# Weight low parts on GpSimd in two halves, softplus high parts on ScalarE, and a rotary table applied earlier, in a two-block transformer kernel

## The chip, the cores and the metric

The kernel runs on 1 core of one Trainium2 chip. The metric is the device time of the whole program in microseconds. Before the change three runs gave 2197.65, 2197.91 and 2201.13 us, a median of 2197.91 us.

## What is computed

Two transformer blocks run one after the other on 512 tokens of width 1024, in float32. Cut to what matters here:

```python
# first block
h = x + 0.5 * swiglu(rms_norm(x))                       # 1024 -> 2816 -> 1024
u = rms_norm(h) @ w_in                                  # q_lat, kv_lat, k_rope, qd, kd, vd
q = (rms_norm(q_lat) @ w_q_up)                          # 8 heads of 64 plain + 32 rotary columns
q_nope = rms_norm(q[..., :64]) ; q_rot = apply_rope(rms_norm(q[..., 64:]), cos, sin)
o_mla = softmax(q @ k.T * scale) @ v                    # first mixer, 8 heads, beside 4 heads of
h = h + concat(o_mla, o_diff) @ w_out                   # difference attention
h = h + 0.5 * swiglu(rms_norm(h)); h = h + gate * rms_norm(p @ w_ple_proj)
# second block, 16 meta tokens ahead of the 512
z = qa @ ka.T * scale                                   # stick breaking, 8 heads
log_keep = where(strict, log_sigmoid(-z), 0)            # = -softplus(z) below the diagonal
a = exp(log_sigmoid(z) + (reverse_cumsum(log_keep) - log_keep)) @ va
# beside it top-k sparse attention, then a mixture of 32 experts, top 2
```

## The kernel before, in words

**Two parts for each factor.** A float32 product is made on TensorE as three products of rounded parts: high by high, high by low and low by high (`mm3`, lines 393 to 397). Each operand is split into a high part, which is the value rounded to the matmul's type, and a low part, which is the value less the high part. For weights this is `wload` (lines 371 to 380): SyncE starts the transfer of a 128 by 1024 block, ScalarE writes the high part (line 376) and GpSimd and VectorE by turns subtract it (line 379). Three raw blocks and three split blocks are held at a time, and `stream` (line 997) loads one weight block ahead of its use. For activations it is `split` (lines 382 to 391).

**Stages.** First feed-forward (to about 385 us of the span), first mixer (to about 720), second feed-forward (to about 1065), a gated projection (to about 1155), second mixer (to about 1600), output projection, and the experts (from about 1670). In a mixer two programs are woven by `merge` (line 1025): the attention, and a stream of projections of 24 products each. A planner then orders the instructions of each engine by program order and by its own estimates of cost and readiness, and puts in the semaphores. Each engine works through its own queue in that order.

**First mixer.** `t_mla` (line 689) projects one pair of heads, gets four tiles `y` from PSUM on VectorE (line 614) and hands three of them to `row_rstd` (line 469), where ScalarE squares them, TensorE sums the squares and VectorE refines the inverse root. Later `mla_n` (line 835) normalises: `kn` (line 840), and for each of the two heads `mqn` (line 848), then the product of its 64 rotary rows with the table `rtab` (line 849), then the split into high part (ScalarE) and low part (GpSimd). The scores follow in `mla_s` (line 856).

**Second mixer.** `sb_a` (line 1359) takes the scores of one head in three groups, two of 512 columns and one of 256. ScalarE copies them (line 1369) and makes Abs, Exp and Ln (lines 1372 to 1374), VectorE adds the positive part (line 1375), GpSimd masks the diagonal blocks (lines 1349 and 1351), VectorE writes the high part (line 1383), GpSimd the low part (line 1384). `sb_b` (line 1390) sums both parts on TensorE (line 1401) and adds the copied scores on VectorE (line 1403). Between these, VectorE runs the top-k of the sparse attention, 64 rounds of a maximum and a replacement (lines 1326 and 1327), woven in by `rank`.

Of the kernel before, what the change touches and what calls it, by code (L numbers as in the profile page):

```python
# [8 lines left out]
F32 = mybir.dt.float32  # L9
F32R = mybir.dt.float32r  # L10
I32 = mybir.dt.int32
AF = mybir.ActivationFunctionType
OP = mybir.AluOpType
# [223 lines left out]
class Prog:  # L237
# [133 lines left out]
    def wload(self, ap, n=1024):  # L371
        nc = self.nc
        raw = self.raw()
        nc.sync.dma_start(raw, ap)
        hl = self.ws.tile([P, 2, 1024], F32R, name="whl", tag="ws")
        nc.scalar.activation(hl[:, 0, :n], raw[:, :n], AF.Copy)  # L376
        e = nc.vector if self.lo_i % 2 else nc.gpsimd
        self.lo_i += 1
        e.tensor_sub(hl[:, 1, :n], raw[:, :n], hl[:, 0, :n].bitcast(F32))  # L379
        return hl  # L380

    def split(self, hl, src, scale=None, rows=slice(0, P), cols=slice(None), lo=None):
# [168 lines left out]
    def block1(self):  # L551
        nc, I = self.nc, self.I
# [17 lines left out]
        rtab = self.U("rtab")  # L570
# [27 lines left out]
        def proj(w, evac=None, src=None, kc=KC, o=0):  # L598
            ps = self.G()
            for k in range(kc):  # L600
                c = slice(o + k * P, o + k * P + P)
                x = (xs if src is None else src)[k]
                self.mm3(ps, w[:, 0, c], w[:, 1, c], x[:, 0, :], x[:, 1, :], k == 0, k == kc - 1)
                if k % 2:
                    yield 1.3
            if evac is None and "rb" not in L_:
                L_["first"] = ps
                return
            evacuate(ps, L_["rb"] if evac is None else evac)
# [6 lines left out]
        def mark(key, lag=0.0):  # L616
            done[key] = self.clock + lag

        def stats(key, items):
            L_[key] = self.row_rstd(items)  # L620
            mark(key, LAG)
# [67 lines left out]
        def t_mla(w, p):  # L689
            if p % 2 == 0:  # L690
                L_["wq"] = w
            ql = [L_["ql", 0], L_["ql", 1]]
            ys = []
            for e in range(2):
                yield from proj(L_["wq"], L_["rbq"], ql, 2, ((2 * p + e) % 4) * 256)
                ys.append(L_["y"])
            for o in (0, 512):
                yield from proj(L_["wkv"], L_["rbkv"], [L_["kvl"]], 1, o + p * P)
                ys.append(L_["y"])
            yield 1.3  # L700
            vd["m", p] = self.U("vm")
            self.transposes(vd["m", p], ys[3])
            Y_["m", p] = ys
            stats(("m", p), [(ys[0], 1), (ys[1], 2), (ys[2], 0)])
            yield 2.0

        def t_wkv(w, _):
# [30 lines left out]
        def need(key):  # L738
            while key not in done or self.clock < done[key]:
                yield None  # L740
# [94 lines left out]
        def mla_n(p):  # L835
            yield from need(("m", p))
            ys, r = Y_.pop(("m", p)), L_["m", p]
            es = [self.pairs(r, 6, o) for o in (4, 0, 2)]
            kn = self.U("kn")
            nc.vector.scalar_tensor_tensor(kn, ys[2], self.g1[:, GMKN : GMKN + 1], self.bc2(es[0]), op0=OP.mult, op1=OP.mult)  # L840
            yield 0.4
            q_["m", p], k_["m", p] = [], []
            for e in range(2):
                rn, rr = slice(64 * e, 64 * e + 64), slice(64 * (1 - e), 64 * (1 - e) + 64)
                k = L_["kt"][e][p % 2]
                self.split(k, kn[rn], rows=rn, lo=nc.gpsimd)
                t = self.U("mqn")
                nc.vector.scalar_tensor_tensor(t, ys[e], gs[:, e : e + 1], self.bc2(es[1 + e]), op0=OP.mult, op1=OP.mult)
                nc.vector.tensor_tensor(t[rr], t[rr], rtab[rr], op=OP.mult)
                q = self.HL("mq")  # L850
                self.split(q, t, lo=nc.gpsimd)
                q_["m", p].append(q)
                k_["m", p].append(k)
                yield 0.4
# [48 lines left out]
        for k in range(2):  # L903
            raw = self.U("praw")
            nc.scalar.dma_start(raw, I["pT"][k])
            hl = self.HL("pT")
# [9 lines left out]
        for h in range(4):  # L916
            for s, f in enumerate((t_q, t_k, t_v)):
                T_["qkv"[s] + str(h)] = [(wA[3 * h + s], lambda w, f=f, h=h: f(w, h))]
            T_[f"m{h}"] = [(I["w_qup"][h // 2] if h % 2 == 0 else None, lambda w, h=h: t_mla(w, h))]
            T_[f"wo{h}"] = [(I["w_out"][h, m4], lambda w, h=h, m4=m4: t_wo(w, h, m4)) for m4 in range(2)]  # L920
# [158 lines left out]
    def mixer2(self):  # L1079
        nc, I = self.nc, self.I  # L1080
# [17 lines left out]
        def need(key):  # L1098
            while key not in done or self.clock < done[key]:
                yield None  # L1100
# [245 lines left out]
        def dmask(t, g):  # L1346
            if g == (1, 3):
                t3 = t.rearrange("p (b c) -> p b c", b=4)[:, 0:4:3, :]
                nc.gpsimd.tensor_tensor(t3, t3, mask.unsqueeze(1).to_broadcast([P, 2, P]), op=OP.mult)
            else:  # L1350
                nc.gpsimd.tensor_tensor(t[:, :P], t[:, :P], mask, op=OP.mult)

        def zmm(z, p, e, j):
            qa, kp = qa_[p], kp_[p]
            r = slice(64 * e, 64 * e + 64)
            kc = slice(j * P, j * P + P)
            self.mm3(z, kp[r, 0, kc], kp[r, 1, kc], qa[r, 0, j * P :], qa[r, 1, j * P :], True, True)

        def sb_a(h):

            p, e = h // 2, h % 2
            yield from need(("ka", p))
            for g in GR:
                w = W[g]
                z = self.PS()
                for j in g:
                    zmm(z[:, OFF[j] : OFF[j] + T - j * P], p, e, j)
                zc = self.U("zc")[:, :w]
                nc.scalar.copy(zc, z[:, :w])
                zz[h, g] = zc  # L1370
                t = self.U("sp")[:, :w]
                nc.scalar.activation(t, z[:, :w], AF.Abs)
                nc.scalar.activation(t, t, AF.Exp, scale=-1.0)
                nc.scalar.activation(t, t, AF.Ln, bias=self.ones)
                nc.vector.scalar_tensor_tensor(t, z[:, :w], 0.0, t, op0=OP.max, op1=OP.add)
                dmask(t, g)
                if w == 512:
                    s = self.HL("spl")
                    hi, lo = s[:, 0, :], s[:, 1, :]
                else:  # L1380
                    s = self.U("splz", 512, F32R)
                    hi, lo = s[:, :256], s[:, 256:]
                nc.vector.tensor_copy(hi, t)
                nc.gpsimd.tensor_sub(lo, t, hi.bitcast(F32))
                for j in g:
                    c = slice(OFF[j], OFF[j] + T - j * P)
                    spl[h, j] = (hi[:, c], lo[:, c])
                yield w * 0.00128
# [167 lines left out]
        def attention():  # L1556
            yield from idx()
            self.tc.keep_in_program_order(nc.scalar.preload_act_table_set("natural_log_exp_and_others"))
            yield from sb_a(0)
            for h in range(8):  # L1560
                p, e = h // 2, h % 2
                g = [sb_a(h + 1)] if h < 7 else []
                g.append(sb_b(h))
                if e == 0 and p:
                    g += [sb_sum(p - 1), sb_o(p - 1)]
                for d in self.zip_(*g):
                    yield d
                    rank(1)
                rank(3)
                if h == 7:  # L1570
                    yield from sb_meta()
            yield from self.zip_(sb_sum(3), sb_o(3))
            yield from sb_meta2()
            rank(80)
            yield from ds_s(0)
            for p in range(4):
                g = [ds_o(p)]
                if p < 3:
                    g.insert(0, ds_s(p + 1))
                if p == 0:  # L1580
                    g.append(sb_out())
                yield from self.zip_(*g)
            self.dump("yb", [t[:, 0, :].bitcast(F32) for t in yb])
# [561 lines left out]
```

## Time and profile before

| | |
|---|---|
| median of three runs | 2197.91 us |
| the profiled execution | 2201.16 us |
| its span, first to last instruction | 2199.3 us |
| mean granted TensorE clock | 0.980 |
| busy: TensorE, VectorE, ScalarE, GpSimd | 2115.3, 1012.4, 707.7, 517.4 us |

Busy time is an average over stages with different limits, so a stage has to be read from its own windows. A busy time includes the time in which an instruction has started and cannot go on. Idle time is put down to the event that came last before it ended. The clock column of a window gives the granted TensorE clock as a share of full speed.

### The profile page before, as it was taken

What the parts mean: (1) busy time and instruction counts of PE and PEld (TensorE: products, weight loads), DVE (VectorE), ACT (ScalarE), POOL (GpSimd) and SP (SyncE); (2) the same over time, 40 slices, a digit from 0 to 9 for tenths busy, and PEclk for the clock granted to TensorE, in tenths of its full rate; (3) what the DMA queues carried; (4) which work ended last, traced back from release to release, by engine and by line L of the source; (5) the groups of instructions that cost most, each with busy time, mean ns of one, the idle gap of its engine ahead of it and who ended that gap; (6) DMA issues with size and microseconds to landing.
All of it is one profiled execution on the core that took longest, in us unless ns stands there. A gap on an engine that the chain in (4) does not pass through costs nothing.

```text
span 2199.3 us, 25719 instructions
## 1 busy us (share of the span) xinstructions
PE 2115.3 (96%) x10225; PEld 1520.7 (69%) x10225; DVE 1012.4 (46%) x1719; ACT 707.7 (32%) x1177; POOL 517.4 (24%) x336
## 2 busy tenths in 40 slices
PE   8999999999899999999989899999999999999997
PEld 6888888777566788888777777667887555445543
DVE  4323235555775542433576996553263232323322
ACT  4222224445554322222444556442231111111111
POOL 3323234323321432323442345111230000000000
PEclk9999999999899999999999999999999999999999
DMA  5333223311011233322321101112626799999993
GB/s 160 96 96 96 96 90 123 102 58 49 10 49 29 87 96 96 96 91 94 120 78 57 49 30 44 39 40 73 229 71 235 321 412 423 409 398 410 412 408 145
DMA packets 67837, 330.72 MB, mean 150 GB/s; under 512 B 7792, under 2 KB 8960, under 8 KB 43648
## 3 DMA queue, kind: packets, MB, share of 16 engines
q1 hardware_dynamic: 66848, 327.45, 40.6%
q8 instruction: 82, 1.34, 0.3%
q10 hardware_dynamic: 864, 1.57, 0.2%
q14 instruction: 43, 0.35, 0.0%
HBM read 326.90 MB, written 2.10 MB: 150 GB/s over the span
## 4 chain that ended last, share of the span: by engine, by line
PE 83%; DVE 9%; ACT 3%; issue 2%; POOL 1%; DMA 1%; SPq 0%; DVEq 0%; ACTq 0%; POOLq 0%
PE pss L1708 10%; PE psg L395 9%; PE psg L397 9%; PE psg L396 9%; PE psg L1708 8%; PE pss L395 4%; PE pss L397 4%; PE pss L396 4%; PE pst L1708 4%; PE pst L396 4%; PE pst L395 4%; PE pst L397 4%; PE pss L410 1%; PE pst L479 1%; PE pst L1713 1%
## 5 line engine op out<-in xcount | busy, mean ns | idle before, releaser
L376 ACT ACTIVATE whl<-wraw 128x1024 fp32r<-128x1024 f32 (+1 forms) x227 | 237.1, 1045 | 663.6 <-PE psg L397 256.5
L379 POOL TENSOR_TENSOR whl<-wraw,whl 128x1024 fp32r<-128x1024 f32 (+1 forms) x114 | 271.6, 2382 | 622.9 <-ACT whl L376 431.1
L379 DVE TENSOR_TENSOR whl<-wraw,whl 128x1024 fp32r<-128x1024 f32 (+1 forms) x113 | 157.5, 1394 | 53.9 <-ACT whl L376 53.9
L2008 POOL TENSOR_TENSOR fr<-fv,mhalf 128x1 f32<-128x1 f32 x4 | 2.2, 546 | 519.5 <-DVE fv L2007 517.1
L1708 PE MATMUL pss<-mw,xe 128*64 128x512 f32 x512 | 115.3, 592 | 0.0
L513 POOL TENSOR_TENSOR t<-t,t 128x512 f32<-128x512 f32 x44 | 58.4, 1327 | 217.1 <-DVE t L512 199.6
L1708 PE MATMUL pss<-mw,hT 128*64 128x512 f32 x480 | 108.0, 603 | 0.6 <-ACT hT L1886 0.5
L1708 PE MATMUL psg<-mw,xe 128*64 128x512 f32 x480 | 108.1, 592 | 0.0
L512 DVE TENSOR_TENSOR t<-pss,rb_f 128x512 f32<-128x512 f32 x44 | 30.4, 691 | 163.3 <-PE pss L397 163.3
L540 DVE SCALAR_TENSOR_TENSOR h<-pst,h 128x512 f32<-128x512 f32 x48 | 33.2, 692 | 134.9 <-PE pst L397 134.8
L1868 DVE SCALAR_TENSOR_TENSOR mt<-pss,sc,mt 128x512 f32<-128x512 f32 x16 | 12.0, 750 | 178.5 <-PE pss L1708 178.5
L1981 DVE TENSOR_TENSOR h<-h,psg 128x512 f32<-128x512 f32 x120 | 81.2, 686 | 22.9 <-PE psg L1708 22.9
L1708 PEld LDWEIGHTS pss<-mw,xe 128*64 128x64 f32 x512 | 36.7, 137 | 73.1 <-issue 73.1
L1708 PEld LDWEIGHTS psg<-mw,xe 128*64 128x64 f32 x480 | 34.3, 137 | 68.2 <-issue 65.0
L391 DVE SCALAR_TENSOR_TENSOR yel<-pss,sc,yeh 128x512 fp32r<-128x512 f32 x32 | 24.0, 751 | 122.0 <-ACT yeh L390 122.0
L1708 PEld LDWEIGHTS pss<-mw,hT 128*64 128x64 f32 x480 | 33.5, 138 | 63.9 <-issue 59.6
L1708 PE MATMUL pst<-disp,uhh 128*128 128x256 f32 x256 | 69.2, 294 | 2.5 <-DVE disp L1786 2.5
L1708 PE MATMUL pst<-disp,uhl 128*128 128x256 f32 x256 | 67.5, 288 | 0.0
L429 POOL TENSOR_TENSOR acc<-acc,sq 128x512 f32<-128x512 f32 x34 | 53.5, 1573 | 46.2 <-ACT sq L428 42.5
L1708 PEld LDWEIGHTS pst<-disp,uhh 128*128 128x128 f32 x256 | 50.1, 196 | 17.1 <-issue 13.1
L1867 ACT ACTIVATE mt<-psg,sc 128x512 f32<-128x512 f32 x16 | 11.0, 687 | 157.1 <-PE psg L1708 134.2
L390 ACT ACTIVATE yeh<-pss,sc 128x512 fp32r<-128x512 f32 x32 | 22.0, 688 | 115.6 <-PE pss L1708 103.3
(882 smaller groups left out, 5670.3 us busy)
## 6 DMA issues: line engine op xcount, KB each, us to landing
mw<-in_w SPq DMA_DIRECT2D x188, 1024.0 KB, 9.4
wraw<-in_w_gu SPq DMA_DIRECT2D x87, 512.0 KB, 3.5
wraw<-in_w_d SPq DMA_DIRECT2D x48, 512.0 KB, 3.5
wraw<-in_w2A SPq DMA_DIRECT2D x38, 512.0 KB, 3.5
wraw<-in_w_inA SPq DMA_DIRECT2D x16, 512.0 KB, 3.5
wraw<-in_w_out SPq DMA_DIRECT2D x8, 512.0 KB, 3.6
wraw<-in_w_pg SPq DMA_DIRECT2D x8, 512.0 KB, 3.5
wraw<-in_w_up SPq DMA_DIRECT2D x8, 512.0 KB, 3.6
```

The costliest lines, as they stand in the source:

```text
L376: nc.scalar.activation(hl[:, 0, :n], raw[:, :n], AF.Copy)
L379: e.tensor_sub(hl[:, 1, :n], raw[:, :n], hl[:, 0, :n].bitcast(F32))
L391: nc.vector.scalar_tensor_tensor(low, src, scale, hi.bitcast(F32), op0=OP.mult, op1=OP.subtract)
L395: mm(ps, whi, xhi, start=first, stop=False)
L396: mm(ps, whi, xlo, start=False, stop=False)
L397: mm(ps, wlo, xhi, start=False, stop=last)
L429: (eng or nc.gpsimd).tensor_add(acc, acc, t)
L512: nc.vector.tensor_tensor(t2, pu, rb, op=OP.mult)
L513: nc.gpsimd.tensor_tensor(t2, t1, t2, op=OP.mult)
L540: nc.vector.scalar_tensor_tensor(self.h[m], py, 0.5, self.h[m], op0=OP.mult, op1=OP.add)
L1708: return self.next_to(nc.tensor.matmul(*args, **kw))
L1981: self.nc.vector.tensor_tensor(self.h[m], self.h[m], ps, op=OP.add)
```

## The change

Three edits. In `wload` the subtraction that falls to GpSimd is issued as two instructions of 512 columns (one of 512 and one of 256 where the block has 768 columns); which blocks go to which engine stays as it was. In `t_mla` the 64 rotary rows of both `y` tiles are multiplied in place by the table, after the statistics were taken from them, and the product is gone from `mla_n`. In `sb_a` the high part is written by ScalarE in place of VectorE.

```diff
@@ wload @@
         nc.scalar.activation(hl[:, 0, :n], raw[:, :n], AF.Copy)
-        e = nc.vector if self.lo_i % 2 else nc.gpsimd
         self.lo_i += 1
-        e.tensor_sub(hl[:, 1, :n], raw[:, :n], hl[:, 0, :n].bitcast(F32))
+        if self.lo_i % 2 == 0:
+            nc.vector.tensor_sub(hl[:, 1, :n], raw[:, :n], hl[:, 0, :n].bitcast(F32))
+            return hl
+        for c in range(0, n, 512):
+            c = slice(c, min(c + 512, n))
+            nc.gpsimd.tensor_sub(hl[:, 1, c], raw[:, c], hl[:, 0, c].bitcast(F32))
         return hl
@@ t_mla @@
             stats(("m", p), [(ys[0], 1), (ys[1], 2), (ys[2], 0)])
+            for e in range(2):
+                rr = slice(64 * (1 - e), 64 * (1 - e) + 64)
+                nc.vector.tensor_tensor(ys[e][rr], ys[e][rr], rtab[rr], op=OP.mult)
             yield 2.0
@@ mla_n @@
-                nc.vector.tensor_tensor(t[rr], t[rr], rtab[rr], op=OP.mult)
                 q = self.HL("mq")
@@ sb_a @@
-                nc.vector.tensor_copy(hi, t)
+                nc.scalar.activation(hi, t, AF.Copy)
                 nc.gpsimd.tensor_sub(lo, t, hi.bitcast(F32))
```

## Rows read from the trace of the kernel before

**Rows 1.** Windows: stretch, length, busy PE, PEld, DVE, ACT, POOL, clock, DMA share, GB/s.

```profile
550.00:605.00 55.00, 45.66 (x205) 31.68 (x204) 40.17 (x92) 29.49 (x65) 17.73 (x14) 0.83 0.03 10
...
1210.00:1265.00 55.00, 48.08 (x292) 42.90 (x292) 51.15 (x101) 28.94 (x59) 20.69 (x21) 0.91 0.15 49
1265.00:1320.00 55.00, 49.96 (x293) 40.24 (x292) 51.81 (x133) 29.69 (x55) 22.97 (x27) 0.97 0.09 30
```

**Rows 2.** Line 1383 by itself: count, ns minimum/median/maximum, first and last start.

```profile
L1383 DVE CAST splh<-sp x16: 416/427/2599, 1231.6 to 1372.3; 128x512 fp32r<-128x512 f32 x16
L1383 DVE CAST splz<-sp x8: 270/294/2440, 1237.4 to 1368.6; 128x256 fp32r<-128x256 f32 x8
```

**Rows 3.** GpSimd in order of time near 1231: start, us, engine, line, operation, tiles.

```profile
1231.48 2.37 POOL L379 TENSOR_TENSOR whl<-wraw,whl 128x1024 fp32r<-128x1024 f32 x1
```

**Rows 4.** TensorE in the second mixer, with idle time before it in brackets.

```profile
1235.14 0.90 PE L548 MATMUL pst<-ident,y2k 128*128 128x128 f32 x3 [2.40 <-DVE y2k L1136]
...
1256.64 0.33 PE L1401 MATMUL pss<-splh,cr 128*128 128x128 f32 x1 [1.54 <-DVE sa L1403]
...
1291.35 0.46 PE L395 MATMUL pss<-qah,kph 64*128 64x512 f32 x1 [2.67 <-DVE sa L1403]
```

**Rows 5.** Windows of three stretches at the lower clock, columns as in rows 1.

```profile
1234.30:1241.10 6.80, 5.96 (x19) 5.27 (x20) 6.66 (x16) 2.23 (x4) 2.39 (x3) 0.50 0.26 77
...
1292.30:1295.70 3.40, 3.40 (x13) 3.21 (x14) 3.31 (x11) 2.12 (x5) 2.04 (x4) 0.50 0.00 0
582.30:589.20 6.90, 3.35 (x8) 2.15 (x9) 3.40 (x3) 3.08 (x7) 6.41 (x5) 0.51 0.00 0
```

**Rows 6.** A ScalarE group of that stage: count | busy us, mean ns | idle before.

```profile
L387 ACT ACTIVATE spmhh<-spm 128x512 fp32r<-128x512 f32 x1 | 0.6, 632 | 0.1
```

**Rows 7.** The rotary product by itself, columns as in rows 2.

```profile
L849 DVE TENSOR_TENSOR mqn<-mqn,rtab x8: 683/1420/1750, 554.3 to 653.9; 64x512 f32<-64x512 f32 x8
```

**Rows 8.** The chain that ended last, start and us, at the second pair of heads.

```profile
580.70 1.58 DVE mqn L849
...
582.30 1.66 DVE mqn L849
```

**Rows 9.** TensorE in the first mixer, idle time before it in brackets.

```profile
556.41 0.79 PE L410 MATMUL pss<-dkh,dqh 64*128 64x512 f32 x1 [1.60 <-DVE mn L767]
...
585.85 1.19 PE L791 MATMUL psg<-at,vd 128*128 128x512 f32 x1 [4.47 <-ACT am L869]
...
614.60 0.51 PE L395 MATMUL pss<-kth,mqh 128*128 128x512 f32 x1 [0.72 <-ACT am L869]
...
657.70 0.50 PE L395 MATMUL pss<-kth,mqh 128*128 128x512 f32 x1 [0.52 <-ACT am L869]
```

**Rows 10.** VectorE in the first mixer, idle time before it in brackets.

```profile
544.00 0.18 DVE L482 TENSOR_SCALAR rv<-pst 128x24 f32<-128x24 f32 x1 [3.61 <-PE pst L479]
...
641.67 0.18 DVE L482 TENSOR_SCALAR rv<-pst 128x24 f32<-128x24 f32 x1 [2.19 <-PE pst L479]
```

**Rows 11.** Two GpSimd subtractions: the page's group, and a line as in rows 2.

```profile
L379 POOL TENSOR_TENSOR whl<-wraw,whl 128x1024 fp32r<-128x1024 f32 (+1 forms) x114 | 271.6, 2382 | 622.9 <-ACT whl L376 431.1
...
L1384 POOL TENSOR_TENSOR spll<-sp,splh x16: 1265/1294/2133, 1234.2 to 1372.8; 128x512 fp32r<-128x512 f32 x16
```

**Rows 12.** VectorE and GpSimd in order of time near 1182.

```profile
1182.25 2.44 DVE L1288 TENSOR_TENSOR qih<-yqi,qih 64x512 fp32r<-64x512 f32 x1 [1.54 <-ACT qih L1287]
...
1181.78 2.37 POOL L379 TENSOR_TENSOR whl<-wraw,whl 128x1024 fp32r<-128x1024 f32 x1 [6.96 <-ACT whl L376]
1184.11 1.73 POOL L1076 TENSOR_TENSOR yqi<-y,rt 128x512 f32<-128x512 f32 x1
```

**Rows 13.** Other VectorE instructions that started beside a weight's low part on GpSimd.

```profile
468.60 1.72 DVE L778 SCALAR_TENSOR_TENSOR cf<-ssum,nlam,cf 128x1 f32<-128x1 f32 x1
...
1135.11 2.37 DVE L494 CAST xs4h<-mg 128x16 fp32r<-128x16 f32 x1
```

**Rows 14.** TensorE at the end of the stick breaking, idle time before it.

```profile
1380.46 2.07 PE L1428 MATMUL psg<-sa,va 128*64 128x512 f32 x7 [1.88 <-POOL sa L1351]
```

More of the change, by code (lines that the diff above doesn't have):

```diff
@@ L843, in mla_n @@
             for e in range(2):
-                rn, rr = slice(64 * e, 64 * e + 64), slice(64 * (1 - e), 64 * (1 - e) + 64)
+                rn = slice(64 * e, 64 * e + 64)
                 k = L_["kt"][e][p % 2]
```

## The prediction, made before the changed kernel was run

> **What bounds the kernel now.** I read the windows by stage first. In the feed-forward and expert stages TensorE has no idle time worth naming, so nothing that the change does on other engines there can move the end. The two mixers are different. From 1210 to 1320 us VectorE is busy for 51.15 and 51.81 of each 55 us, and TensorE for 48.08 and 49.96 at a mean clock of 0.91 and 0.97 [rows 1]. From 550 to 605 us TensorE works 45.66 of 55 us at 0.83 [rows 1]. So there are two kinds of loss to win back: idle TensorE, and TensorE at the lower of its two levels, 1.2 in place of 2.4 GHz. In a stretch at the lower level a matmul that is there to be done takes about twice as long, so half of the stretch is lost.
>
> The second look was at VectorE in order of time, for instructions of one shape with very different durations. The softplus cast of 128 by 512 has a minimum of 0.416, a median of 0.427 and a maximum of 2.599 us, that of 256 columns 0.270, 0.294 and 2.440 [rows 2]. The long ones stand at the same moments as a weight's low part of 2.37 us on GpSimd [rows 3], and end when it ends: VectorE and GpSimd exclude each other for the whole of an instruction. There are three such casts, and TensorE sat idle for 2.40, 1.54 and 2.67 us behind VectorE right after them [rows 4]. Each idle time was followed by a stretch at the lower level, of 6.8, 3.4 and 3.4 us (the first and the third are shown, the second is like the third) [rows 5].
>
> **Part 1, the high part on ScalarE.** VectorE loses 24 casts, 16 of 0.427 and 8 of 0.294 us, which is 9.2 us, and the waits of the three long ones, 2.17 + 2.17 + 2.15 = 6.5 us. ScalarE gets 24 copies. The same shape and types take 0.632 us there [rows 6], and 256 columns between 0.3 and 0.42 us, my estimate from half of that and the whole less a fixed part; together about 16 x 0.63 + 8 x 0.38 = 13.2 us. ScalarE is busy for 29 to 30 of 55 us in this stage [rows 1], so there is room, and the chain of one group becomes 0.2 us longer. On the path to the end: VectorE came 2.4 to 2.6 us earlier at the three places, which covers the idle times of 2.40, 1.54 and 2.67, sum 6.6 us. If TensorE isn't idle there, the clock may stay up: the three stretches lose 13.6 / 2 = 6.8 us, of which I count half, 3.4, since the rows don't show which part of the idle time brings the clock down. All of it is 10.0 us. The change adds a wait: the copy waits on ScalarE for the mask on GpSimd, and behind it stand the next group's copy out of PSUM, its Abs, Exp and Ln, the exponential of line 1404 and the high parts of weights. VectorE had the same wait, with the top-k and the PSUM evacuations behind it.
>
> **Part 2, the table at the projection.** Eight products leave the way from `mqn` to the scores. They took between 0.683 and 1.750 us, in the median 1.420 [rows 7]; the short ones met nothing on GpSimd. In the chain that ended last they are the pieces ahead of the longest idle time of TensorE in the first mixer: 1.58 + 1.66 = 3.24 us [rows 8] before 4.47 us of idleness [rows 9]; the high part on ScalarE waits for them, and the copy that TensorE needs stands behind that high part. At the first pair two short ones (1.4 us) end before an idle time of 1.60 [rows 9]. At the third and fourth pair four each time, 0.72 to 0.52, eight idle times in all with a sum of 5.2 us, lie within such a chain (the first and the last are shown) [rows 9], and the products there take up to 1.75 us each. What can be won is the smaller of each two numbers: 1.4 + 3.2 + 5.2 = 9.8 us, and 1.7 us as half of what the lower clock of 6.9 us after the long idleness costs [rows 5]: 11.5 us. The eight products come back at the projection, at 8 x 0.69 = 5.5 us. I cost them at nothing, because VectorE waits there for the sums of the squares: 3.6 us at the first and 2.2 us at the fourth pair (the first and last of four such waits) [rows 10], and a pair needs 1.4. If the planner puts them behind the refinement of the inverse root instead, this cover is gone, they stand in the chain again, and what is won at the last two pairs falls from 5.2 us to the 0.5 to 1 us of each that was waiting for GpSimd, about 3 us in all.
>
> **Part 3, halves on GpSimd.** The whole takes 2.382 us, one of 512 columns 1.265 to 1.294 [rows 11], so two halves take 2.56 and GpSimd is 0.2 us later with each of 114 blocks. TensorE hardly ever waits for these low parts, since the blocks are loaded one ahead. What changes is how long VectorE is shut out: 1.3 us at most in place of 2.4, if VectorE gets in between. The trace has an example of two GpSimd instructions in a row: a VectorE instruction that began at 1182.25 ended 0.5 us after the first of them, and the second took 1.73 us, some 0.45 more than its 1.27 [rows 11, 12]. So VectorE did get in between. Instructions in VectorE's chain that were held by a weight are of the kind of lines 778 and 494 (1.72 us for one element in a row, 2.37 us for 16) [rows 13]; I find seven such in the chain with idle TensorE after them, and each would end about 1 us sooner: 7 us, of which I count half, because in some a second VectorE instruction then meets the second half. Against it stand two places where TensorE waits for what follows a weight on GpSimd, one of them with 1.88 us [rows 14]: 0.2 us each, and with the clock perhaps 0.5. Net 3.0 us; its bounds are a loss of 3 and a gain of 7.
>
> The Trainium skill, GPSIMD Engine Reference, 2.1 Instruction dispatch, warns that consecutive Pool instructions are no barrier between its cores, and that a core starts on the next as soon as its own share is done. By that the two halves could hold VectorE out as one instruction of 2.56 us, and this part would lose where I count a gain. The trace speaks for a change of hands between two instructions, in the one example above.
>
> **The sum.** If every idle time closed: 10.0 + 11.5 + 3.0 = 24.5 us. I take two thirds, 16 us. That share is a choice and not read from a row: TensorE works in order, and an idle time that closes only moves on to the engine that is late next. That is GpSimd in the second mixer (mask and low parts) and ScalarE in the first. The ends are nothing and all, with another 3 us if all of the clock comes back. The profiled execution took 2201.16 us, of which 2199.3 are its span and 1.9 lie around it; that makes 2185 for it. It is 3.3 us above the median of the runs shown, and against the median of 2197.91 the forecast is 2182.
>
> **The rivals.** (a) Less than half: the idle times close but the clock stays down, and each closes by half. Then 3.3 + 4.9 + 0 = 8 us, 2190. For it: the mean clock of 0.83 from 550 to 605 us [rows 1] is far lower than one stretch of 6.9 us explains, so in part it falls without a long idleness. Against it: at 1234 and 1292 the stretch begins right at one. (b) Nothing: in the second mixer VectorE runs the top-k rounds in all gaps, so that its queue stays full, the planner puts the moved products behind the refinement, and 0 to 4 us are left: 2194 to 2199, taken at 2197. Against it: the top-k is a fixed amount of work. (c) Slower: ScalarE's copy waits for the mask when the mask stands behind a weight's low part on GpSimd, and TensorE's scores wait for the PSUM copies behind it. One such case costs what a long cast costs now, some 2.4 us and 1.7 to 3.4 of clock, so 4 to 6 us. Five weights fall to GpSimd while the 24 groups run. With three such cases part 1 is undone, and from five on, 20 to 30 us against 14.5 of the other two parts, the kernel is slower: about 2205. For it: ScalarE's queue is in order and feeds TensorE directly. Against it: the same mask stood before the cast on VectorE, and the group's idle time before it was short. (d) The halves hold VectorE out as one instruction: seven instances of 0.2 us and the two places lose 2 us in place of the 3 won, and two thirds of 10.0 + 11.5 are left, less 2: 12 us, 2186. (e) The change doesn't do what it says, because the product of 64 rows in place waits for the squares and delays what stands behind it on VectorE: that is the loss of cover priced in part 2, and lies within (a) and (b).
>
> **How the numbers follow.** Forecast 0.50, (a) 0.22, (b) 0.12, (c) 0.10, (d) 0.06. Below 0.2%, which is 4.4 us and about what a measurement of this kernel can tell from no change, the result counts as the same. The forecast, (a) and (d) are faster, less 0.01 for their upper ends: 0.77. Same is most of (b), 0.12, and slower is (c) and the rest, 0.11. The range starts at 2170, where all idle times close and the clock comes back (24.5 + 3.4 less than the median), and ends at 2198, so that it holds the forecast, (a), (d) and most of (b).
>
> **What would show it right or wrong.** Right: no VectorE instruction of `sb_a` above 0.7 us, no idle TensorE above 1 us near the former 1235, 1256 and 1291, and the clock of that stage at 0.97 or more; the idle time of 4.47 us below 1.5, and the moved products near 0.69 us each, before the refinement; VectorE instructions beside a weight on GpSimd held for 1.3 us at most. Wrong: ScalarE idle before the new copy for over 1 us in more than three groups, with TensorE idle behind it; the products in the chain at their new place; VectorE held for 2.5 us by two halves; or a different order on the queues with idle times at new places that eat the gain.

## The result, and the profile after

The changed kernel takes 2172.19 us, the median of four runs (2171.27 to 2172.92), beside 2197.78 us for the kernel before in the same set. The ratio is 0.9876, 95% interval 0.9863 to 0.9888: 25.6 us faster. The forecast was 2182, 16 us faster, in a range of 2170 to 2198. The direction was right and the time lies in the range, but the gain is 1.6 times the forecast.

The profiled execution took 2171.27 us, its span is 2169.4 us and its mean granted clock 0.989 (0.980 before). First the busy times from its page:

```profile
PE 2103.2 (97%) x10225; PEld 1511.6 (70%) x10225; DVE 959.2 (44%) x1695; ACT 719.0 (33%) x1201; POOL 550.8 (25%) x450
```

VectorE is busy for 53 us less than before (1012.4 us). The 24 casts that left it were 9.2 us of work. The rest is time in which it was held: over all its instructions, the time above the shortest of the same shape fell from 177 to 131 us. Next, windows around the two mixers, for before and then after. The stretches of after are set to the same work, by the starts of the same ScalarE instructions. The columns are those of rows 1.

```profile
385.00:740.00 355.00, 330.42 (x1629) 244.11 (x1628) 217.26 (x453) 168.14 (x332) 104.09 (x67) 0.96 0.16 51
1090.00:1500.00 410.00, 377.65 (x2007) 291.69 (x2006) 290.72 (x616) 198.53 (x385) 137.07 (x118) 0.96 0.16 51
```

```profile
385.00:728.00 343.00, 327.68 (x1632) 242.81 (x1631) 209.97 (x454) 168.40 (x333) 108.91 (x83) 0.98 0.17 53
1077.00:1476.00 399.00, 372.68 (x2001) 286.14 (x2000) 274.44 (x591) 209.64 (x408) 141.53 (x136) 0.97 0.17 53
```

A window's length less TensorE's busy time is its idle time. In the first mixer that was 24.6 us and is 15.3; in the second 32.3 and 26.3. So 15.3 us of idleness went. TensorE's busy time for the same work fell by 2.7 and 5.0 us, which is the clock: its stretches at the lower level in the two windows fell from 61.4 to 34.2 us. Together 23.0 us. The spans differ by 29.9 us. The other 6.9 lie behind 1660 us, where the experts run: the trace of before has three stretches there at the lower clock, 17.0 us in all, that of after one of 3.4, and half of the difference is 6.8. It isn't shown to be an effect of the change: the experts' code is the same in all kernels of this study, their traces have 3.4 to 17.0 us of it, and two traces of the changed kernel 3.4 and 10.2. It may also be why the profiled executions stand 29.9 us apart and the medians 25.6.

The windows that answer to rows 1 (shifted to the same work):

```profile
548.00:603.00 55.00, 49.20 (x241) 35.22 (x242) 40.25 (x104) 31.10 (x70) 18.07 (x16) 0.96 0.03 10
1194.00:1249.00 55.00, 49.90 (x323) 42.99 (x321) 52.40 (x113) 33.47 (x67) 23.10 (x26) 1.00 0.16 49
1247.00:1302.00 55.00, 52.37 (x302) 40.96 (x301) 51.85 (x153) 35.61 (x67) 26.29 (x30) 1.00 0.13 39
```

The clock went from 0.83, 0.91 and 0.97 to 0.96, 1.00 and 1.00 [rows 1]. VectorE is as full as before. In the two windows of the second mixer the top-k fills what became free, with 20 and 40 rounds where 15 and 30 stood; the first window has no top-k and holds more of VectorE's other work.

Now TensorE in order of time, with its idle time before each row in brackets:

```profile
579.23 1.10 PE L798 MATMUL psg<-at,vd 128*128 128x512 f32 x2 [1.18 <-DVE at L1069]
...
1133.24 0.59 PE L400 MATMUL psg<-xs5l,whl 128*128 128x264 f32 x1 [1.75 <-DVE xs5l L499]
1136.80 0.59 PE L399 MATMUL psg<-xs6h,whl 128*128 128x264 f32 x1 [2.75 <-ACT xs6h L394]
...
1201.64 0.39 PE L1308 MATMUL pss<-kih,qih 128*128 128x264 f32 x1 [1.99 <-DVE qih L1294]
1219.08 0.33 PE L1407 MATMUL pss<-spll,cr 128*128 128x128 f32 x1 [0.72 <-POOL spll L1390]
...
1318.96 0.51 PE L1407 MATMUL pss<-spll,cr 128*128 128x512 f32 x1 [2.08 <-POOL spll L1390]
```

The idle time of 4.47 us is 1.18 now [rows 9]. Those of 2.40, 1.54 and 2.67 us [rows 4] are gone: nothing above 0.80 us is left near the three places. A new one of 2.08 us has come, behind GpSimd. The places at 1133, 1137 and 1202 us stay; they had 1.75, 3.05 and 2.10 us before.

The moved pieces, as in rows 2: first the high parts on ScalarE, with what ScalarE waited for before them and which of TensorE's two queues waited for them (total us, times), then the product at its new place.

```profile
L1389 ACT ACTIVATE splh<-sp x16: 615/632/637, 1215.3 to 1351.5; 128x512 fp32r<-128x512 f32 x16
L1389 ACT ACTIVATE splz<-sp x8: 400/418/419, 1219.5 to 1347.0; 128x256 fp32r<-128x256 f32 x8
its engine sat idle before it (us, times) until:
  POOL sp L1357: 16.7, 12
  POOL sp L1355: 9.7, 7
...
  PEld pss L1407: 1.5, 3
  PE pss L1407: 0.4, 2
```

```profile
L711 DVE TENSOR_TENSOR y<-y,rtab x8: 678/886/1642, 540.8 to 629.1; 64x512 f32<-64x512 f32 x8
```

ScalarE stood idle for 26.4 us, in 19 waits, for the mask on GpSimd. No wait in the trace is put down to the product.

### The profile page after: what moved, and what is told of

Read it like the earlier page. It is cut to its first block, busy times and chain, and to the rows that moved or that the text cites. A ratio compares the mean times of both kernels' runs of the same rounds, so it can differ in the third digit from the quotient of the medians.

```text
span 2169.4 us, 25890 instructions
## 1 busy us (share of the span) xinstructions
PE 2103.2 (97%) x10225; PEld 1511.6 (70%) x10225; DVE 959.2 (44%) x1695; ACT 719.0 (33%) x1201; POOL 550.8 (25%) x450
## 4 chain that ended last, share of the span: by engine, by line
PE 83%; DVE 8%; ACT 3%; issue 2%; POOL 2%; DMA 1%; SPq 0%; DVEq 0%; POOLq 0%; ACTq 0%
PE pss L1714 10%; PE psg L399 10%; PE psg L401 9%; PE psg L400 9%; PE psg L1714 8%; PE pss L399 4%; PE pss L401 4%; PE pss L400 4%; PE pst L400 4%; PE pst L399 4%; PE pst L401 4%; PE pst L1714 4%; PE pss L414 1%; PE pst L483 1%; PE pst L1719 1%
## 5 line engine op out<-in xcount | busy, mean ns | idle before, releaser
L383 POOL TENSOR_TENSOR whl<-wraw,whl 128x512 fp32r<-128x512 f32 x228 | 307.0, 1367 | 613.2 <-ACT whl L376 379.0
L514 DVE TENSOR_TENSOR t<-psg,rb_f 128x512 f32<-128x512 f32 x44 | 30.4, 691 | 82.2 <-PE psg L401 76.7
```

The source lines that it names most:

```text
L383: nc.gpsimd.tensor_sub(hl[:, 1, c], raw[:, c], hl[:, 0, c].bitcast(F32))
L514: nc.vector.tensor_tensor(t1, pg, rb, op=OP.mult)
```

## The experiments

All times are medians, beside runs of the kernel before on the same chip. A per cent of the time is 22 us.

**One part at a time.** Three kernels carry one part of the change each. The first is the copy on ScalarE:

```diff
-                nc.vector.tensor_copy(hi, t)
+                nc.scalar.activation(hi, t, AF.Copy)
```

> Only the softplus high part on ScalarE; weights whole and the rotary product in its old place. Theory A (what counts is the mutual exclusion of VectorE and GpSimd, and idle TensorE behind the three long casts): the idle times of 2.40, 1.54 and 2.67 us fall below 0.8 each and most of the three stretches at the lower clock go, so 7 to 11 us less than before, 2187 to 2191. Rival L (the 9.2 us of VectorE work matter, not the three waits): a gain of the same size, but spread, with idle TensorE still above 1.5 us at one of the three places. Rival S (ScalarE waits for the mask, which stands behind a whole weight on GpSimd): under 4 us, with new idle times of TensorE of over 1.5 us behind ScalarE.

Measured: 2195.47 beside 2199.46 us, ratio 0.9977 (0.9966 to 0.9988), 3 to 7 us won where the sum had 10.0. That is less than theory A and about the bound of rival S, whose new idle times came too, but behind GpSimd and not behind ScalarE. The three held casts are gone, and with them the three idle times. One new one stands close to the second of the three places, and two more 47 and 79 us behind the third (TensorE, after what ScalarE waited for):

```profile
  POOL sp L1351: 18.6, 12
  POOL sp L1349: 9.7, 7
...
1254.80 0.38 PE L1401 MATMUL pss<-splz,cr 128*128 128x256 f32 x1 [1.66 <-POOL splz L1384]
...
1338.42 0.50 PE L1401 MATMUL pss<-spll,cr 128*128 128x512 f32 x1 [1.96 <-POOL spll L1384]
...
1370.10 0.38 PE L1401 MATMUL pss<-splz,cr 128*128 128x256 f32 x1 [1.41 <-POOL splz L1384]
```

The chain of a group runs mask, high part, low part, and two of the three are GpSimd's. Where its weight stands before the mask or the low part, the group is late whoever writes the high part. By the engine whose event ended it, TensorE's idle time from 1085 to 1495 us went from 21.0 to 15.7 us behind VectorE, and from 5.4 to 8.8 behind GpSimd.

The second is the rotary table at the projection:

```diff
             stats(("m", p), [(ys[0], 1), (ys[1], 2), (ys[2], 0)])
+            for e in range(2):
+                rr = slice(64 * (1 - e), 64 * (1 - e) + 64)
+                nc.vector.tensor_tensor(ys[e][rr], ys[e][rr], rtab[rr], op=OP.mult)
...
-                nc.vector.tensor_tensor(t[rr], t[rr], rtab[rr], op=OP.mult)
```

> Only the rotary product at the projection. Theory A (the chain of VectorE from the normalisation to the scores gets shorter, and the products find VectorE waiting at their new place): 10 to 14 us less than before, 2184 to 2188, the offset won between 550 and 720 us, the idle time of 4.47 us below 1.5. Rival P (cover lost, the products stand behind the refinement of the inverse root): 3 to 7 us less.

Measured: 2189.03, ratio 0.9950 (0.9937 to 0.9963), 8 to 14 us. ScalarE's instructions are 3.0 us early at 575 us and 8 to 9 early from 636 us on. This is the place of the 4.47 us, which are 1.10 here, and the first mixer's idle time falls from 24.6 to 18.0 us.

The third is the two halves alone. VectorE's blocks stay whole:

```diff
-        e.tensor_sub(hl[:, 1, :n], raw[:, :n], hl[:, 0, :n].bitcast(F32))
...
+        for c in range(0, n, 512):
+            c = slice(c, min(c + 512, n))
+            nc.gpsimd.tensor_sub(hl[:, 1, c], raw[:, c], hl[:, 0, c].bitcast(F32))
```

> Only the GpSimd halves. Theory A (VectorE gets in between two halves): VectorE instructions beside a weight are held for 1.3 us at most, also the casts, which take 1.7 at most; 4 to 9 us less than before, 2189 to 2194. Rival H (the halves shut VectorE out as one instruction): holds of up to 2.5 us remain, 0 to 3 us more than before.

Measured: 2188.09, ratio 0.9950 (0.9928 to 0.9971), 6 to 16 us, where the sum had 3.0. The interval is wide because its ten runs lie in two groups, near 2182 and near 2196 us, with granted clocks of 0.985 to 0.989 and 0.978 to 0.982. So the median stands for neither group, and why an execution falls into one or the other isn't shown. The trace is one of 2182.26 us: it is 12.5 us early at 1645 us, and the rest lies in the experts. The casts, still on VectorE, were held for half as long [rows 2]:

```profile
L1387 DVE CAST splh<-sp x16: 426/428/1503, 1223.5 to 1360.1; 128x512 fp32r<-128x512 f32 x16
L1387 DVE CAST splz<-sp x8: 271/294/1367, 1228.2 to 1356.4; 128x256 fp32r<-128x256 f32 x8
...
1368.37 3.25 PE L1432 MATMUL psg<-sa,va 128*64 128x512 f32 x14 [2.02 <-POOL sa L1355]
```

The last row is the cost that the prediction named: 1.88 us became 2.02 [rows 14], a loss of 0.14. In the changed kernel this idle time is gone. A second loss of the same size is 1.22 us behind ScalarE near 1440 us, which became 1.37 (1.35 in the changed kernel).

**The changed kernel, varied.** Its softplus cast back on VectorE, which leaves parts 2 and 3:

```diff
-                nc.scalar.activation(hi, t, AF.Copy)
+                nc.vector.tensor_copy(hi, t)
```

> The changed kernel with the softplus high part back on VectorE: halves and rotary product stay. Theory A2 (after the halves a cast is held for 1.1 us at most, and ScalarE's new wait for the mask gives back most of what is left): within 4 us of the changed kernel, 2170 to 2177, casts of at most 1.7 us. Rival W (the copy on ScalarE is worth its 7 us beside the other two as well): 2178 to 2183, with idle TensorE of over 1.3 us behind a held cast at two places or more.

Measured: 2175.64, ratio 0.9903 (0.9890 to 0.9917) beside 0.9876: the copy on ScalarE is worth some 6 us by the ratios and 3.5 by the medians. The time is that of theory A2, but rival W's sign is there too: two of the three idle times are back, at 1.31 and 1.42 us.

Work added to VectorE: a maximum over 288 or 144 columns after each high part.

```diff
                 nc.scalar.activation(hi, t, AF.Copy)
+                nc.vector.tensor_reduce(self.S("dum", 1), t[:, : w // 2 + w // 16], axis=AX.X, op=OP.max)
```

> The changed kernel with one VectorE maximum over 288 of 512 (144 of 256) columns of the masked softplus in each of the 24 groups, whose result nobody uses: about 0.4 and 0.25 us each, the work and the wait for the mask that the cast had on VectorE, but reading one tile only and writing one column. Theory A (the exclusion counts): within 3 us of the changed kernel, 2172 to 2175. Rival L (VectorE's work and its wait for the mask count): 5 to 9 us more than the changed kernel, 2177 to 2181.

Measured: 2170.44, ratio 0.9869 (0.9851 to 0.9886), no slower than the changed kernel. The added work is that of the casts which the change took away:

```profile
L1390 DVE TENSOR_REDUCE dum<-sp x24: 277/452/455, 1215.2 to 1349.7; 128x1 f32<-128x288 f32 x16, 128x1 f32<-128x144 f32 x8
```

So no price of the 9.2 us of VectorE's work is to be seen. But one reading is left open: the planner orders this kernel anew, with some 390 of TensorE's 10225 instructions at another place than in the changed kernel, so what the work costs could be hidden by what the new order gives. The copy itself changes the order as well. The five kernels of this study with the cast on VectorE have one order in the second mixer, to within some 25 instructions, and the kernels with the copy on ScalarE, but for this one, have another, some 330 away. With it the idle time of 1.88 us at 1380 us [rows 14] goes, a gain that the prediction had not counted; in the five it stays at 1.63 to 2.03. How much of what the copy wins comes from holds that are gone, and how much from the new order, is not separated; the last kernel below speaks for the holds.

The moved products left out, so that the first mixer's rotary rows are not turned at all:

```diff
-            for e in range(2):
-                rr = slice(64 * (1 - e), 64 * (1 - e) + 64)
-                nc.vector.tensor_tensor(ys[e][rr], ys[e][rr], rtab[rr], op=OP.mult)
```

> The changed kernel with the eight rotary products left out altogether, so that the first mixer's rotary rows are not turned. Theory A (the moved products find VectorE waiting): within 2 us of the changed kernel, 2170 to 2174. Rival P (they stand in a chain at their new place): 4 to 6 us less than the changed kernel.

Measured: 2171.39, ratio 0.9867 (0.9851 to 0.9882). The products cost nothing that can be measured at their new place.

The meta columns, whose VectorE casts and subtractions stand before the idle times at 1133 and 1137 us, given to ScalarE and GpSimd:

```diff
-            nc.vector.tensor_copy(hi, self.mg[:, m, :])
-            nc.vector.tensor_sub(lo, self.mg[:, m, :], hi.bitcast(F32))
+            nc.scalar.activation(hi, self.mg[:, m, :], AF.Copy)
+            nc.gpsimd.tensor_sub(lo, self.mg[:, m, :], hi.bitcast(F32))
```

> The changed kernel with the 16 meta columns of the second block's input made by ScalarE (high part) and GpSimd (low part) in place of VectorE, eight pairs of small instructions. Theory A (these small VectorE instructions, 0.16 us alone, are held for 1.1 us each at four places of a stage in which TensorE waits for VectorE): 2 to 6 us less than the changed kernel, 2166 to 2170, with the idle times of 1.75 and 2.76 us near 1133 and 1137 shorter. Rival N (that stage is bound by the chain of products and sums of the gate): within 2 us.

Measured: 2174.73, ratio 0.9882 (0.9867 to 0.9897), no gain. The two idle times there, 1.75 and 2.75 us, became 0.75 and one of 4.37:

```profile
1135.54 1.67 DVE L985 TENSOR_TENSOR h<-h,pu 128x512 f32<-128x512 f32 x1
...
1138.03 0.59 PE L399 MATMUL psg<-xs6h,whl 128*128 128x264 f32 x1 [4.37 <-ACT xs6h L394]
```

The first became 1.0 us shorter, as theory A had it. Then the sum `h`, which took 0.69 us in the changed kernel, starts just after the next weight's low part has begun on GpSimd and is held for 1 us, and ScalarE's `xs6h` waits for it. The hold fell on another instruction, and nothing was won.

**Shorter still, and why halves help.** The low part in four instructions of 256 columns:

```diff
-        for c in range(0, n, 512):
-            c = slice(c, min(c + 512, n))
+        for c in range(0, n, 256):
+            c = slice(c, c + 256)
```

> The changed kernel with GpSimd's weight low parts in instructions of 256 columns, four for a block. Theory A (VectorE is held for one GpSimd instruction): holds by a weight of 0.75 us at most, 1 to 5 us less than the changed kernel, 2167 to 2171. Rival O (each GpSimd instruction costs its own fixed time, four take 2.94 us, and TensorE or the masks behind them wait): 0 to 5 us more, 2172 to 2177.

```profile
L383 POOL TENSOR_TENSOR whl<-wraw,whl x448: 719/738/2305, 11.4 to 1625.3; 128x256 fp32r<-128x256 f32 x150
```

Measured: 2169.77, ratio 0.9864 (0.9849 to 0.9879). It is the lowest median of all, 2.4 us under the changed kernel, but the intervals overlap, so it isn't shown to be better. Beside a weight no VectorE instruction is held for over 0.7 us in its trace but one, for 1.09.

The last four kernels ran on one chip beside one set of runs of the kernel before (2199.55 us). The changed kernel again is the mark:

> The changed kernel once more, as the mark for the three others of this set. Both theories: ratio to the kernel before 0.986 to 0.989, 24 to 30 us less.

Measured: 2172.21, ratio 0.9870 (0.9854 to 0.9887).

The weight's low part whole again, with parts 1 and 2 as they are:

```diff
-        for c in range(0, n, 512):
-            c = slice(c, min(c + 512, n))
+        for c in (slice(0, n),):
```

> Parts 1 and 2 without the halves: the GpSimd low part is one instruction of 1024 columns again. If the three parts win at separate places, the sum of the single ones holds: 5 + 11 = 16 us less than before, 11 us slower than the changed kernel. If the ScalarE copy and the halves win partly at the same places (the three long casts), the halves are worth less beside it: 5 to 8 us slower than the changed kernel. L379 at 2.38 us again, and VectorE instructions of little work held for up to 2.2 us.

Measured: 2188.23, ratio 0.9944 (0.9930 to 0.9957), 16 us above the mark. Both numbers expected were too low: beside the other two parts the halves are worth 16 us, at least what they won alone. The traces agree: at 1645 us, before the experts, this kernel is 11.7 us early and the mark 26.0. And parts 1 and 2 together win 12 us where part 2 alone won 11, so the copy on ScalarE is worth about 1 us as long as the weights stay whole, which these intervals can't tell from nothing.

The same number of GpSimd instructions as with halves, but cut so that the first stays long:

```diff
-        for c in range(0, n, 512):
-            c = slice(c, min(c + 512, n))
+        for c in (slice(0, n - 64), slice(n - 64, n)):
```

> All three parts, but the GpSimd low part is cut into 960 and 64 columns: as many instructions and waits as with the halves, and nearly the long hold of the whole (about 2.25 us). Theory H, the halves win because VectorE is held for a shorter time: as slow as the kernel without halves, 5 to 11 us above the changed kernel, and holds of up to 2.1 us in its trace. Theory O, they win because a second instruction changes the planner's order or lets the reader of the first part begin sooner: within 2 us of the changed kernel.

Measured: 2181.39, ratio 0.9908 (0.9893 to 0.9922). That lies between the two, 9.2 us above the mark and 6.8 below the whole, and neither theory alone gives it. The order of the instructions on TensorE, VectorE and ScalarE is the same in this kernel as in both others, but for ten of TensorE's 10225 instructions and one of VectorE's; two traces of the changed kernel differ by five. So a new order is not the reason. Three traces at the same two places, rows of TensorE, VectorE and GpSimd in order of time. First the whole:

```profile
1141.74 2.64 POOL L382 TENSOR_TENSOR whl<-wraw,whl 128x1024 fp32r<-128x1024 f32 x1 [2.41 <-ACT whl L376]
1144.34 1.26 POOL L432 TENSOR_TENSOR acc<-acc,sq 128x512 f32<-128x512 f32 x1
1144.34 1.81 DVE L394 SCALAR_TENSOR_TENSOR xs6l<-h,g,xs6h 128x512 fp32r<-128x512 f32 x1
1146.20 0.59 PE L399 MATMUL psg<-xs6l,whl 128*128 128x264 f32 x1 [1.77 <-DVE xs6l L394]
...
1244.18 2.38 POOL L382 TENSOR_TENSOR whl<-wraw,whl 128x1024 fp32r<-128x1024 f32 x1 [0.87 <-ACT whl L376]
1246.52 0.78 POOL L1389 TENSOR_TENSOR splz<-sp,splz 128x256 fp32r<-128x256 f32 x1
1247.36 0.39 PE L1406 MATMUL pss<-splz,cr 128*128 128x256 f32 x1 [1.67 <-POOL splz L1389]
```

Then 960 and 64 columns:

```profile
1141.29 2.79 POOL L382 TENSOR_TENSOR whl<-wraw,whl 128x960 fp32r<-128x960 f32 x2 [2.41 <-ACT whl L376]
1143.75 0.87 DVE L394 SCALAR_TENSOR_TENSOR xs6l<-h,g,xs6h 128x512 fp32r<-128x512 f32 x1
1144.03 1.73 POOL L432 TENSOR_TENSOR acc<-acc,sq 128x512 f32<-128x512 f32 x1
1144.68 0.59 PE L399 MATMUL psg<-xs6l,whl 128*128 128x264 f32 x1 [0.69 <-DVE xs6l L394]
...
1238.06 2.25 POOL L382 TENSOR_TENSOR whl<-wraw,whl 128x960 fp32r<-128x960 f32 x1 [0.88 <-ACT whl L376]
1240.27 0.78 POOL L1389 TENSOR_TENSOR splz<-sp,splz 128x256 fp32r<-128x256 f32 x1
1241.02 0.31 POOL L382 TENSOR_TENSOR whl<-wraw,whl 128x64 fp32r<-128x64 f32 x1
1241.11 0.39 PE L1406 MATMUL pss<-splz,cr 128*128 128x256 f32 x1 [1.53 <-POOL splz L1389]
```

Then halves (the second run of the changed kernel):

```profile
1230.81 1.30 POOL L383 TENSOR_TENSOR whl<-wraw,whl 128x512 fp32r<-128x512 f32 x1 [0.87 <-ACT whl L376]
1232.06 0.79 POOL L1390 TENSOR_TENSOR splz<-sp,splz 128x256 fp32r<-128x256 f32 x1
1232.81 1.29 POOL L383 TENSOR_TENSOR whl<-wraw,whl 128x512 fp32r<-128x512 f32 x1
1232.91 0.39 PE L1407 MATMUL pss<-splz,cr 128*128 128x256 f32 x1 [0.58 <-POOL splz L1390]
```

Two things are to be seen. First, a boundary by itself is worth something. In the whole, the subtraction `xs6l` starts when the weight ends, together with the next long GpSimd instruction `acc`, and VectorE, which had just been held by the weight, is held a second time: 1.81 us. With the small piece in between it takes 0.87, TensorE waits 0.69 in place of 1.77, and `acc` is the one that takes longer, 1.73 in place of 1.26. Secondly, the length counts, and not for VectorE alone: at the second place GpSimd takes the softplus low part between the two pieces of the weight, and TensorE, which waits for just that, stands idle for 1.67, 1.53 and 0.58 us. This second form is rare, two of 114 blocks in the changed kernel; the rest of the length's effect I put down to VectorE's holds. Summed over the VectorE instructions of the two mixers that ran beside a weight, the time above the shortest of the same shape (where it is over 0.2 us) is about 32, 29 and 20 us in the three kernels, with a longest single hold of 2.22, 2.08 and 1.16 us.

The last kernel asks whether the copy on ScalarE is needed at all when the holds are short: quarters, with the cast on VectorE.

```diff
-        for c in range(0, n, 512):
-            c = slice(c, min(c + 512, n))
+        for c in range(0, n, 256):
+            c = slice(c, c + 256)
...
-                nc.scalar.activation(hi, t, AF.Copy)
+                nc.vector.tensor_copy(hi, t)
```

> Parts 2 and 3 with the GpSimd low part in four instructions of 256 columns, and the softplus high parts on VectorE. Theory H: no cast is held over 0.7 us beyond its own 0.43, the three idle times of TensorE shrink to under 1 us, and the kernel is within 2 us of the changed one without the ScalarE copy. Rival: the copy on ScalarE is worth its 3 to 6 us whatever the hold, because it also frees 9 us of VectorE: then 3 to 6 us slower than the changed kernel.

```profile
L1389 DVE CAST splh<-sp x16: 427/428/945, 1212.4 to 1347.2; 128x512 fp32r<-128x512 f32 x16
L1389 DVE CAST splz<-sp x8: 269/294/816, 1217.0 to 1343.5; 128x256 fp32r<-128x256 f32 x8
```

Measured: 2173.73, ratio 0.9878 (0.9862 to 0.9895), 1.5 us above the mark and within its interval. With halves in place of quarters the same order of instructions took 2175.64 us, and of the two idle times of 1.31 and 1.42 us there 0.77 and 0.87 are left. So most of what the copy wins beside halves can be had by shorter holds, as far as ratios whose intervals just overlap (0.9903 and 0.9878) can tell. Beside quarters (2169.77 us) the copy may still be worth 3 to 4 us, which the intervals don't show.

TensorE's idle time in the traces of these kernels, from windows of 350 us (385 to 735) and 410 us (1085 to 1495), each less its busy time:

| kernel | first mixer | second mixer | sum | median us |
|---|---|---|---|---|
| before | 24.6 | 32.3 | 56.9 | 2197.8 to 2199.6 |
| copy on ScalarE alone | 24.7 | 30.5 | 55.2 | 2195.47 |
| halves alone | 23.0 | 28.2 | 51.2 | 2188.09 |
| rotary alone | 18.0 | 32.4 | 50.4 | 2189.03 |
| copy and rotary, weights whole | 18.0 | 31.2 | 49.2 | 2188.23 |
| all three, cut at 960 | 16.9 | 27.2 | 44.1 | 2181.39 |
| rotary and halves | 15.4 | 27.7 | 43.1 | 2175.64 |
| the changed kernel, two traces | 15.3, 14.0 | 26.1, 25.0 | 41.4, 39.0 | 2172.2 |
| quarters, cast on VectorE | 13.8 | 25.3 | 39.0 | 2173.73 |

The idle times are each of one execution, for the halves alone of one near 2182 us. The times follow the idle time, with 1.4 to 2.0 us of time for each us of it, and 2.3 for the copy alone, where the 1.7 us of idle time are too few to tell. What goes beyond one fits the clock, whose share in the changed kernel was 7.7 of 23.0 us above.

## Why the prediction was right in sign and short in size

**What bounds the kernel: right.** Compared instruction by instruction (the high parts of the weights on ScalarE), the changed kernel is 0.4 us early at 386 us, 12.1 at 696, 13.3 at 1133, 23.7 at 1390 and 23.8 at 1645. Nearly all of it comes from the two mixers and the gated projection just before the second.

**Part 1, 10.0 us: wrong in size.** It won 3 to 7 us alone, about 1 beside part 2 with whole weights, 3.5 to 6 in the changed kernel. The terms on VectorE were right: no high part above 0.637 us and the three idle times gone. The failed step is that they would close without a successor. The prediction named the successor itself, GpSimd, in the argument for its share and in rival (c). Its sign for that was seen by half: ScalarE is idle for over 1 us before 17 of the 24 copies, but TensorE for over 0.5 us behind only three of them (0.72, 0.56 and 2.08), and for over 1 us behind three where the copy stood alone (1.41 to 1.96). So the wait is common and seldom on the path. What the step did not have at all is the new order, and with it the 1.88 us that went.

**Part 2, 11.5 us: right.** It won 8 to 14 alone. The products take 0.68 to 1.64 us at their new place, with a median of 0.886 where I had 0.69 for each, and leaving them out changes nothing, as the cover said. The cover was thinner than the prediction had it: of the four waits that it counted on, one (at 606 us) was only 0.33 us. And two of the products stand inside the refinement of the first pair, between its start at 544.18 and its next step at 545.78:

```profile
544.39 1.46 DVE L711 TENSOR_TENSOR y<-y,rtab 64x512 f32<-64x512 f32 x2
```

That they cost nothing even there was not foreseen. The 4.47 us became 1.18. The clock term of 1.7 us was read too large: of the 6.9 us at the lower level TensorE worked only 3.35 [rows 5], so the lower level cost some 1.7 us there, and half of that is 0.8.

**Part 3, 3.0 us: the worst step, too small by far.** It won 6 to 16 us alone, 16 beside the other two. Three things went wrong in it. I had counted seven held instructions in the chain and then halved their 7 us, because a second VectorE instruction might meet the second half. That does happen (`qil` behind `qih`):

```profile
1167.16 1.36 DVE L1294 TENSOR_TENSOR qih<-yqi,qih 64x512 fp32r<-64x512 f32 x1 [1.56 <-ACT qih L1293]
1168.56 1.65 DVE L1294 TENSOR_TENSOR qil<-yqi,qil 64x512 fp32r<-64x512 f32 x1
```

The second had this row before:

```profile
1184.72 1.65 DVE L1288 TENSOR_TENSOR qil<-yqi,qil 64x512 fp32r<-64x512 f32 x1
```

The first is down from 2.44 us [rows 12], and the second was held for as long before the change, by the next GpSimd instruction, so nothing was lost by it. Then, I counted the halves as pure cost for GpSimd, 0.2 us for each block. Others in the same queue gain as well, such as the low parts of the softplus: with parts 1 and 2 in place, TensorE's idle time behind GpSimd in the two mixers went from 9.8 us with wholes to 8.4 with halves. And part 3 had no clock to win back, while parts 1 and 2 had. The bounds of -3 to +7 did not hold the value, because they were drawn from the same seven places.

**Two thirds: about right for parts 1 and 2.** The full sum was 24.5 us, and 25.6 were measured. The share of two thirds was a choice, argued by GpSimd being late next. It was about right for parts 1 and 2 alone: 10.0 + 11.5 = 21.5, two thirds are 14, and 12 were measured. What the forecast lacks is part 3, of which two thirds are 2 us where 16 were measured beside the other two. Part 3 also shortens GpSimd's instructions, and so takes back some of what the share was for. That the full sum comes out right is in large part luck, a part 1 too large against a part 3 too small.

**The rivals.** (a) and (b) fall with the time. (c) is met above: its mechanism is there, its price was too high. (d), halves that hold VectorE as one instruction, falls. Those beside a weight are held for 1.16 us at most. The Trainium skill, SBUF — State Buffer, Who interferes with whom, says of a VectorE instruction in a 2-port mode that whoever issues first holds the pair of ports that the two engines share for the whole instruction. The traces agree in the length of the hold: casts took up to 2.599, 1.503 and 0.945 us beside GpSimd instructions of 1024, 512 and 256 columns, and 0.427 us when not held. Which mode they run in, no trace shows. The longest holds of any VectorE instruction beside a weight were 2.22, 2.08 and 1.16 us for 1024, 960 and 512 columns. The warning of the Trainium skill, GPSIMD Engine Reference, 2.1 Instruction dispatch, which I had made into rival (d), does not show here as a longer hold. (e) falls with the kernel without products.

**The signs.** Clock of the former 1210 to 1320 us at 0.97 or more: 1.00. The 4.47 us below 1.5: yes. Holds at 1.3 us at most: yes. No VectorE instruction of `sb_a` above 0.7 us: 0.692 at most. Products near 0.69 us and before the refinement: in part, as said under part 2. No idle TensorE above 1 us near the three places: true for the places, but 2.08 us came later in the same mixer, at 1317 us.

**Left open.** How the 16 us of part 3 divide between VectorE's holds and GpSimd's own queue is shown at the places above, and by the engine whose event ended TensorE's idle time in the two mixers: from wholes to halves it falls by 8.1 us behind VectorE (29.1 to 21.0) and by 1.4 behind GpSimd. What the clock adds to each is not known. What of the 6.8 us between the whole and the cut at 960 is the boundary, and what the 0.14 us of shorter hold, was not taken apart. Neither was the new order that comes with the copy on ScalarE.

## What to carry to other kernels

Where VectorE instructions of one shape show very different durations, look at what GpSimd runs beside them, and make that instruction shorter before moving the victims elsewhere: here the cut alone won 6 to 16 us, and moving 24 victims 1 to 7. Cost a shorter instruction for every waiter, its own engine's queue among them, and not as added overhead alone. A share for "what is late next" has to be checked against the other parts of the change, since one of them may take back some of it. And where a planner orders the instructions, compare their order before a difference is put down to the edit alone.

## What the runs showed of the hardware that I had not expected

- A held VectorE instruction is let in at the boundary between two GpSimd instructions, even when the second is as short as 0.3 us, and that turn saved 0.94 us of VectorE (1.81 to 0.87).
- The maximum over columns on VectorE was never held: 24 of them took 0.277 to 0.455 us. Three of these began some 0.1 us after a weight's half on GpSimd and took 0.454, 0.305 and 0.452 us; in the kernel with the cast back on VectorE, casts that began so took up to 1.500.
